# Chunk 3 of both second feed-forward nets by seven block products, with its sums of weights made in DRAM

## The chip, the cores and the metric

The kernel runs on one core of a Trainium2 chip. The metric is the device time of one execution in microseconds; lower is better. [...] In this kernel SP issues most transfers and POOL the accumulating ones, which add what they read to what lies at their destination. Each engine works through its own instructions in the order in which the program put them.

## The reference

Two layers over 256 tokens of width 1024, in 32-bit floats. Each layer runs a feed-forward net, a mixer, a cross attention over 256 memory rows and a second feed-forward net, with a layer norm behind each:

```python
def swiglu(x, w_gate, w_up, w_down):
    return (jax.nn.silu(x @ w_gate) * (x @ w_up)) @ w_down

for l in range(DEPTH):                      # DEPTH = 2, D_FF = 2816
    h = layer_norm(ALPHA * h + 0.5 * swiglu(h, ffn1_gate[l], ffn1_up[l], ffn1_down[l]), ...)
    z = h @ w_in[l]
    ...                                     # gated convolution, linear recurrence, pooling
    h = layer_norm(ALPHA * h + mix, ...)
    h = layer_norm(ALPHA * h + cross_attn(h, mem, ca_q[l], ca_k[l], ca_v[l], ca_o[l]), ...)
    h = layer_norm(ALPHA * h + 0.5 * swiglu(h, ffn2_gate[l], ffn2_up[l], ffn2_down[l]), ...)
```

The change concerns `ffn2`, of both layers: gate and up are 1024 x 2816, down is 2816 x 1024. A part of the mixer's work is issued beside it.

## The kernel before

**Splits.** A product in 32-bit floats is made as three matmuls of a rounded format: each operand is split into a high and a low part, and high x high, high x low and low x high are added up in PSUM. Weights arrive in pieces of 128x1024 (512 KB) in a ring of six buffers `raw`; ScalarE rounds a piece to `whi` (line 75), VectorE subtracts that from it to get `wlo` (line 76). There are eight buffers of each. Activations are split in the same way (`xT`, `kTh`, `ah` and their low parts).

**A feed-forward net** (`ffn`) takes the 2816 columns in six chunks: 0 to 4 are 512 wide, chunk 5 is 256 wide. A chunk makes gate and up for all 256 tokens, the activation and their product, transposes that (`turn`, through a transfer `dealt`), and its rows of `down` follow later in two slabs of 24 matmuls into the accumulators `dn` (`both`). The list `later` says how many slabs stand behind each chunk.

A chunk is made in one of two ways. `hidden` is the plain one: 96 matmuls of 128x512 and eight pieces of weights. `by_seven` cuts tokens and depth into halves, and gate and up into two depth halves each (`w00` = upper half of gate, `w01` = upper half of up, `w10` and `w11` the lower halves), and makes the four results from seven block products of 12 matmuls each instead of eight: X00 by w00, four sums of blocks of x (`bx`, made once for a net) by sums of weight blocks or by a block, X01 by w10 and X11 by a sum of all. It is 84 matmuls, but 14 pieces of weights to split. The sums of weights are made in place, by additions on VectorE (line 702) and by accumulating transfers that POOL issues (`more`, line 738). Where the pieces lie is said by `homes`: two of the blocks use spare buffers, so that they are loaded early, the others the ring `raw`. `put` adds or subtracts a result in PSUM and a tile in SBUF on VectorE, `taken` copies a result by ScalarE, and `between` are slabs of `down` that stand between the products. Which chunks are made so stands in `sevens` (line 821): chunks 2 and 4 in the first net of layer 0, 2, 4 and 5 in the other three.

**The mixer** runs between the first net and the attention. It makes `f`, the keys `k` of the recurrence from it, values, gates, and windows of the pooling (`pw`), whose rims POOL sets to zero (line 1252), and at the end of the recurrence two powers of mean squares `ss` on POOL (line 1219), each followed by a scaled result `yr` (line 1226) that is transposed for the last product of the mixer. In the mixer POOL has nothing else to issue.

What sets the order is the order of the code, apart from `tc.issue_after(x)`, which puts what is written under it behind the instruction x. A transfer waits, on the engine that issues it, for its buffer to be free and for what it reads to be there; what stands behind it in that engine's queue waits with it.

Of the kernel before, what the change touches and what calls it, by code (L numbers as in the profile page):

```python
# [60 lines left out]
def model(ctx: ExitStack, tc: tile.TileContext, t: dict, out: bass.AP):  # L61
# [4 lines left out]
    ps = ctx.enter_context(tc.tile_pool(name="ps", bufs=4, space=PSUM))  # L66

# [257 lines left out]

    squares = kTh[:, 4:8, :].rearrange("p k c -> p (k c)")
# [149 lines left out]
    def ffn(l, name, n, pend=None, last=False, early=None, started=None, following=None):  # L476
        gate, up, down = (t[f"{name}_{x}"][l] for x in ("gate", "up", "down"))
        with tc.tile_pool(name="ffn", bufs=2, reuse_waits="tile") as fp:
# [186 lines left out]
            def by_seven(c0, ncol, bx, between):  # L665
# [22 lines left out]
                if ncol == CHUNK:  # L688
                    homes = [("spare0", "spare1"), ("lng", "lnb"), ("raw", "raw")]
                    n = sevens.index(c0 // CHUNK)  # L690
                    homes = [homes[(n + i) % 3] for i in range(3)] + [("spare2", "raw")]
                else:
                    homes = [("spare2",), ("raw",), ("raw",), ("raw",)]
                w00 = block(gate, 0, pieces(*homes[0]))
                w01 = block(up, 0, pieces(*homes[1]))
                w10 = block(gate, 1, pieces(*homes[3]))
# [23 lines left out]
                def put(o, a, op, b):  # L720
                    nc.vector.tensor_tensor(ordered(o), in_order(a), ordered(b), op=op)
# [18 lines left out]
                o = [bank() for _ in range(3)]  # L740
                run(o[0], part_of_x(0, 0), parts_of(w00))
                taken(s[:, 0, :], o[0])
                run(o[1], bx[0], parts_of(w00, w01))
                more(w01, up, 1)
                run(o[2], part_of_x(0, 1), parts_of(w10))
                between[0]()
                put(s[:, 0, :], o[2], ALU.add, s[:, 0, :])
                w11 = block(up, 1, pieces(*homes[2]))
                run(o[0], bx[1], parts_of(w00, w11), True)
                if ncol == CHUNK:  # L750
                    more(w00, gate, 1)
                copied = taken(e, o[0])
                between[1]()
                nc.scalar.activation(s[:, 0, :], s[:, 0, :], AF.Silu)
                put(e, o[1], ALU.subtract, e)
                if ncol == CHUNK:
                    run(o[0], bx[2], parts_of(w01), True)
                    taken(f, o[0])
                    o.append(bank())
                    run(o[3], bx[3], parts_of(w11))  # L760
                    put(f, o[1], ALU.subtract, f)
                    run(o[0], part_of_x(1, 1), parts_of(w00), True)
                else:
                    o.append(bank())
# [696 lines left out]
```

## Time and profile before

| | |
|---|---|
| median of the runs | 1063.58 us (1063.55 to 1064.38) |
| span of the profiled execution, first to last instruction | 1061.1 us |
| what the median has beyond the span | 2.5 us |
| TensorE busy | 1051.2 us, 99% |
| VectorE busy | 933.2 us, 88% |
| ScalarE busy | 662.0 us, 62% |
| GpSimd busy | 94.7 us, 9% |
| bytes moved by DMA | 251.06 MB, 237 GB/s in the mean |

The second net of layer 0 lies from 372.8 to 539.7 us of the span, that of layer 1 in the last 166 us. In it chunk 2 lies at 406.5 to 435, chunk 3 at 435 to 466, chunk 4 at 466 to 494.5, and chunk 5 with the last slabs at 494.5 to 520.4; these are read from TensorE's matmuls. The mixer of layer 0 lies about 174 to 290 us.

Rows of a timeline read: start, length, engine, line, operation, output<-input with sizes, count, and in brackets the idle time before and what ended it. Rows of a stretch list the busy time of each engine in it, the clock granted to TensorE (1.00 is full speed), the share of time that the DMA engines were busy, and GB/s. Matmuls overlap in the pipeline, so what one costs is the distance between starts, not the listed length.

### The profile page before, as it was taken

The page shows a single profiled execution, that of the slowest core. Times are in us where ns is not written, and L with a number is a line of the kernel's source. Part 1 is how long each engine was busy: PE and PEld are TensorE (multiplying, and loading weights), DVE is VectorE, ACT ScalarE, POOL GpSimd, SP SyncE. Part 2 cuts the span into 40 slices and gives each one's busy share as a digit, 9 for nine tenths or more (in the row PEclk, how much of TensorE's full clock was granted, in tenths as well). Part 3 has the DMA queues.
Part 4 walks back from the last instruction along what each step waited for, and adds up shares of the span by engine and source line. Part 5 has one row for each costly group of instructions (what it writes and reads, how often), then busy time and mean ns, then how long its engine had stood idle before and what let it go on. Part 6 is the DMA issues. An engine that isn't in the chain of part 4 may idle for free.

```text
span 1061.1 us, 16496 instructions
## 1 busy us (share of the span) xinstructions
PE 1051.2 (99%) x6014; PEld 934.8 (88%) x6014; DVE 933.2 (88%) x1246; ACT 662.0 (62%) x909; POOL 94.7 (9%) x128
## 2 busy tenths in 40 slices
PE   9999999999999999999999999999999999999996
PEld 7888888889899888889888888998998998888896
DVE  6998898989988789887898987999899787898787
ACT  6675775676557566655665656666774655675661
POOL 8002001000000001010001001010000000000001
PEclk9999999999999999999999999999999999999999
DMA  9999984854675589988789978866636675799971
GB/s 364 296 320 280 260 272 146 268 166 155 210 271 179 171 281 231 363 192 217 239 305 254 338 224 208 271 233 222 206 122 215 241 243 162 242 303 294 241 194 68
DMA packets 142306, 251.06 MB, mean 237 GB/s; under 512 B 11249, under 2 KB 51985, under 8 KB 142225
## 3 DMA queue, kind: packets, MB, share of 16 engines
q1 hardware_dynamic: 130656, 228.89, 65.0%
q0 software_dynamic: 10992, 19.94, 10.9%
q10 hardware_dynamic: 576, 1.18, 0.3%
q8 instruction: 47, 0.77, 0.3%
q14 instruction: 35, 0.28, 0.1%
HBM read 234.50 MB, written 1.05 MB: 222 GB/s over the span
## 4 chain that ended last, share of the span: by engine, by line
PE 92%; DVE 3%; DMA 2%; issue 2%; ACT 1%; POOL 0%; DVEq 0%; ACTq 0%; POOLq 0%
PE acc L132 61%; PE dn L132 27%; DVE wlo L76 2%; PE acc L199 1%; DMA raw<-in_ffn_gate_dram 1%; DMA raw<-in_ffn_down_dram 1%; ACT whi L75 0%; PE dn L1139 0%; DVE raw L702 0%; PE dn L1213 0%; DMA lng<-in_ln_g_dram 0%; DMA h<-in_x_dram 0%; DVE al L76 0%; PE acc L581 0%; DVE square L531 0%
## 5 line engine op out<-in xcount | busy, mean ns | idle before, releaser
L75 ACT CAST whi<-raw 128x1024 fp32r<-128x1024 f32 (+1 forms) x452 | 456.1, 1042 | 201.2 <-PE dn L132 58.0
L76 DVE TENSOR_TENSOR wlo<-raw,whi 128x1024 fp32r<-128x1024 f32 (+1 forms) x452 | 534.5, 1211 | 53.1 <-ACT whi L75 47.1
L132 PE MATMUL acc<-whi,xT 128*128 128x512 f32 (+1 forms) x1064 | 313.9, 372 | 0.0
L132 PEld LDWEIGHTS acc<-whi,xT 128*128 128x128 f32 x1064 | 199.0, 189 | 26.9 <-DVE xT L76 0.3
L132 PE MATMUL acc<-wlo,xT 128*128 128x512 f32 (+1 forms) x532 | 197.9, 372 | 0.0
L132 PE MATMUL dn<-whi,ah 128*128 128x512 f32 x346 | 131.5, 380 | 0.0
L132 PE MATMUL dn<-wlo,ah 128*128 128x512 f32 x346 | 131.3, 379 | 0.0
L132 PE MATMUL dn<-whi,al 128*128 128x512 f32 x346 | 131.1, 379 | 0.0
L132 PE MATMUL acc<-xT,whi 128*128 128x512 f32 x480 | 117.6, 381 | 0.0
L132 PEld LDWEIGHTS acc<-wlo,xT 128*128 128x128 f32 x532 | 100.6, 189 | 13.4
L132 PEld LDWEIGHTS acc<-xT,whi 128*128 128x128 f32 x480 | 86.8, 190 | 9.8
L132 PE MATMUL dn<-whi,xT 128*128 128x512 f32 x288 | 87.7, 380 | 0.0
L132 PEld LDWEIGHTS dn<-wlo,ah 128*128 128x128 f32 x346 | 65.4, 189 | 9.6 <-DVE wlo L76 0.6
L132 PEld LDWEIGHTS dn<-whi,al 128*128 128x128 f32 x346 | 65.4, 189 | 9.2
L132 PEld LDWEIGHTS dn<-whi,ah 128*128 128x128 f32 x346 | 65.4, 189 | 9.0
L132 PEld LDWEIGHTS acc<-xT,wlo 128*128 128x128 f32 x480 | 62.9, 191 | 3.2
L132 PE MATMUL acc<-xT,wlo 128*128 128x256 f32 x480 | 63.2, 275 | 0.0
L132 PE MATMUL acc<-wlo,kTh 128*128 128x512 f32 (+1 forms) x176 | 61.7, 351 | 0.0
L132 PE MATMUL acc<-whi,kTl 128*128 128x512 f32 (+1 forms) x176 | 61.7, 351 | 0.0
L132 PE MATMUL acc<-whi,kTh 128*128 128x512 f32 (+1 forms) x176 | 61.7, 351 | 0.0
L132 PEld LDWEIGHTS dn<-whi,xT 128*128 128x128 f32 x288 | 54.4, 189 | 7.6
L132 PE MATMUL dn<-wlo,xT 128*128 128x512 f32 x144 | 54.6, 379 | 0.0
(252 smaller groups left out, 1296.8 us busy)
## 6 DMA issues: line engine op xcount, KB each, us to landing
raw<-in_ffn_up_dram SPq DMA_DIRECT2D x88, 512.0 KB, 5.7
raw<-in_ffn_down_dram SPq DMA_DIRECT2D x88, 512.0 KB, 5.6
raw<-in_ffn_gate_dram SPq DMA_DIRECT2D x84, 512.0 KB, 5.6
raw<-in_w_in_dram SPq DMA_DIRECT2D x48, 512.0 KB, 4.8
dealt<-sg SPq DMA_DIRECT2D x80, 128.0 KB, 4.5
raw<-in_ffn_up_dram POOLq DMA_DIRECT2D x19, 512.0 KB, 6.3
raw<-in_ffn_gate_dram POOLq DMA_DIRECT2D x16, 512.0 KB, 9.4
raw<-in_ca_k_dram SPq DMA_DIRECT2D x16, 512.0 KB, 5.2
```

The costliest lines, as they stand in the source:

```text
L75: rounded = nc.scalar.copy(hi, src)
L76: lows.append(nc.vector.tensor_tensor(lo, src, hi.bitcast(F32), op=ALU.subtract))
L132: turns.append(nc.tensor.matmul(o, w, x, start=start, stop=stop, skip_group_check=more))
L199: turns.append(nc.tensor.transpose(pt[:, k, :], src[:, (4 * j + k) * P : (4 * j + k + 1) * P], unit))
```

## The change

Three things are done.

- Chunk 3 of `ffn2` in both layers is made by seven products (`sevens` becomes (2, 3, 4, 5) there). Its four sums of weights (gate0 + up0; up0 + up1; gate0 + up0 + up1; that and gate1) are made in DRAM, in tiles `sum` of 256x512, by transfers that POOL issues: eight copies and four accumulating transfers behind the making of `k` early in the mixer (a small copy `mark` ties them to it), four more behind the memsets of `pw`. In chunk 3 SP then loads 14 pieces, eight of them from `sum`, all by the ring of six. It needs no additions on VectorE and no accumulating transfer of its own.
- In all products by seven X01's product is accumulated by TensorE on top of X00's. ScalarE copies the first product to a second bank, `total`, on which three other products accumulate, and later writes `total` times -1 to a fourth bank, `less`, on which the last sum by w11 accumulates. Two of four additions on VectorE fall away in each; the subtraction f = e - total now reads the bank that TensorE goes on accumulating in.
- In `ffn2` no slab of `down` stands behind a chunk any more (`later` is all 0): the two that stood behind chunk 3 stand inside it. The buffers of chunk 4 in `ffn2` are those that chunk 2 has.

The core of the diff:

```diff
+    def weight_sums(l, name, c):
...
+        def copies():
+            for n, (m, j) in enumerate(((gate, 0), (up, 0), (gate, 0), (gate, 1))):
+                for i in range(2):
+                    nc.gpsimd.dma_start(spread(made[n][i]), part(m, j, i))
+
+        def adds(n):
+            for i in range(2):
+                src = part(up, n, i) if n < 2 else spread(made[n - 1][i])
+                nc.gpsimd.dma_start(spread(made[n][i]), src, accum_op=ALU.add)
+    def after(x, do):
+        mark = sm.tile([P, 8], F32, tag="mark", name="mark", bufs=1)
+        with tc.issue_after(nc.gpsimd.tensor_copy(mark, x).ins):
+            do()
...
+                def summed(n):
+                    to = pieces("raw", "raw")
+                    for x, y in zip(to, stored[n]):
+                        loads.append(nc.sync.dma_start(x, spread(y)))
+                    return to
...
-                    n = sevens.index(c0 // CHUNK)
+                    n = 1 if c0 == 4 * CHUNK and ready is None else 0
...
-                o = [bank() for _ in range(3)]
-                run(o[0], part_of_x(0, 0), parts_of(w00))
-                taken(s[:, 0, :], o[0])
-                run(o[1], bx[0], parts_of(w00, w01))
-                more(w01, up, 1)
-                run(o[2], part_of_x(0, 1), parts_of(w10))
+                o, total, one = (bank() for _ in range(3))
+                run(o, part_of_x(0, 0), parts_of(w00))
+                nc.scalar.copy(total, o)
+                if stored:
+                    run(one, bx[0], parts_of(summed(0)))
+                    w10 = block(gate, 1, pieces(*homes[3]))
+                else:
+                    run(one, bx[0], parts_of(w00, w01))
+                taken(e, one)
+                if not stored:
+                    more(w01, up, 1)
+                run(o, part_of_x(0, 1), parts_of(w10), True)
                 between[0]()
-                put(s[:, 0, :], o[2], ALU.add, s[:, 0, :])
-                w11 = block(up, 1, pieces(*homes[2]))
-                run(o[0], bx[1], parts_of(w00, w11), True)
-                if ncol == CHUNK:
+                activate(s, 0, o)
+                if stored:
+                    run(total, bx[1], parts_of(summed(2)), True)
+                else:
+                    w11 = block(up, 1, pieces(*homes[2]))
+                    run(total, bx[1], parts_of(w00, w11), True)
+                if ncol == CHUNK and not stored:
                     more(w00, gate, 1)
-                copied = taken(e, o[0])
+                less = bank()
+                copied = nc.scalar.mul(less, total, -1.0)
                 between[1]()
...
+                if stored:
+                    run(total, bx[2], parts_of(summed(1)), True)
+                    put(f, e, ALU.subtract, total)
+                    run(less, bx[3], parts_of(block(up, 1, pieces(*homes[2]))), True)
+                    run(total, part_of_x(1, 1), parts_of(summed(3)), True)
+                elif ncol == CHUNK:
+                    run(total, bx[2], parts_of(w01), True)
+                    put(f, e, ALU.subtract, total)
+                    run(less, bx[3], parts_of(w11), True)
+                    run(total, part_of_x(1, 1), parts_of(w00), True)
                 else:
...
+            after(k[:, 0, 0, 0:8], lambda: (ready[1](), ready[2](0), ready[2](1)))
...
+                cleared = nc.gpsimd.memset(x[:, :, 0:PAD], 0.0)
+            with tc.issue_after(cleared.ins):
+                ready[2](2)
+                ready[2](3)
...
+        ready = weight_sums(l, "ffn2", 3)
+        pend = mixer(l, lambda: keys(l, 1), ready)
```

Two places show what moves. The first is GpSimd's queue in the mixer of layer 0; `pw0` and `pw1` are the rims of the pooling windows, `ss` the two powers, `sum` the tiles in DRAM. Before:

```order
L1252 MEMSET pw0_2720 128x2x16
L1219 TENSOR_TENSOR ss_2614<-ss_2614,nhalf_71 128x4
L1252 MEMSET pw1_2721 128x2x16
L1219 TENSOR_TENSOR ss_2660<-ss_2660,nhalf_71 128x4
```

and now, from the last of the accumulating transfers of the first group on (the `mark`, the eight copies and three more of these stand ahead of it):

```order
L351 DMA sum_1811<-in_ffn2_up_dram 128x2x512
L1307 MEMSET pw0_2740 128x2x16
L1274 TENSOR_TENSOR ss_2634<-ss_2634,nhalf_73 128x4
L1307 MEMSET pw1_2741 128x2x16
L351 DMA sum_1812<-sum_1810 128x2x512
L351 DMA sum_1813<-sum_1811 128x2x512
L1274 TENSOR_TENSOR ss_2680<-ss_2680,nhalf_73 128x4
L351 DMA sum_1814<-sum_1812 128x2x512
L351 DMA sum_1815<-sum_1813 128x2x512
```

Two sums of sums now stand between the second memset and the second power; they wait for `sum_1810` and `sum_1811`, which the accumulating transfers of the first group end, and for the copies into their own tiles.

The second is VectorE's queue at the end of chunk 4 of `ffn2` in layer 0, from the splits of the last block on; `halves` holds e and f, the `raw` that is added to is a piece of chunk 5. Before:

```order
L76 TENSOR_TENSOR wlo_4942<-raw_4712,whi_4941 128x1024
L721 TENSOR_TENSOR halves_4725<-acc_4727,halves_4725 128x512
L76 TENSOR_TENSOR wlo_4946<-raw_4713,whi_4945 128x1024
L76 TENSOR_TENSOR wlo_4974<-raw_4963,whi_4973 128x1024
L702 TENSOR_TENSOR raw_4963<-raw_4963,raw_4965 128x1024
L76 TENSOR_TENSOR wlo_4992<-raw_4963,whi_4991 128x1024
L721 TENSOR_TENSOR halves_4725<-acc_4727,halves_4725 128x512
L76 TENSOR_TENSOR wlo_5009<-raw_4967,whi_5008 128x1024
L721 TENSOR_TENSOR halves_4725<-acc_4919,halves_4725 128x512
```

and now:

```order
L77 TENSOR_TENSOR wlo_4991<-raw_4763,whi_4990 128x1024
L77 TENSOR_TENSOR wlo_4995<-raw_4764,whi_4994 128x1024
L77 TENSOR_TENSOR wlo_5023<-raw_5012,whi_5022 128x1024
L747 TENSOR_TENSOR raw_5012<-raw_5012,raw_5014 128x1024
L766 TENSOR_TENSOR halves_4776<-halves_4776,acc_4778 128x512
L77 TENSOR_TENSOR wlo_5041<-raw_5012,whi_5040 128x1024
L766 TENSOR_TENSOR halves_4776<-halves_4776,acc_4911 128x512
```

The first of the three additions to `halves` is gone (ScalarE's copy of e takes its place), and f, the first row of `halves` now, stands behind the two splits of the last block (`raw_4763` and `raw_4764`, to which the accumulating transfers of w00 add), a chunk-5 split and a raw addition, as it did but for one split. It now reads `total`, the bank in which TensorE's last run goes on.

65 lines of the change are left out of this document (34 added, 31 removed).

## The prediction

> **What bounds the kernel now.** I read the page first: the busy times, then the slices, then the chain of work that ended last, then the timelines of single engines in the stage that is changed.
>
> ```profile
> PE 1051.2 (99%) x6014; PEld 934.8 (88%) x6014; DVE 933.2 (88%) x1246; ACT 662.0 (62%) x909; POOL 94.7 (9%) x128
> 372.79 41.44 PE acc L132 x192
> 414.23 5.18 PE dn L132 x24
> 519.21 1.15 DVE wlo L76
> 520.40 7.17 PE dn L132 x32
> ```
>
> The first row says that TensorE is busy for 99% of the span, and VectorE for 88%. The other four are pieces of the chain (start, length, what). In the second feed-forward net of layer 0 the chain runs along TensorE: 192 matmuls in 41.44 us are 0.2158 us each, 24 in 5.18 us are 0.2158 as well. Here a matmul taken out is time taken out, as long as the other engines keep up. The last two rows are the warning: at 519.21 the chain passes to a VectorE subtraction (a `wlo`), and TensorE goes on at 520.40 only when that is done. At the end of this net VectorE delivers just in time.
>
> ```profile
> 406.50:435.00 28.50, 28.50 (x133) 24.95 (x132) 27.31 (x28) 20.23 (x23) 2.38 (x2) 1.00 1.06 317
> 435.00:466.00 31.00, 31.00 (x145) 27.16 (x144) 25.93 (x26) 15.71 (x18) 2.38 (x2) 1.00 0.91 268
> 466.00:494.50 28.50, 28.50 (x135) 24.96 (x134) 22.48 (x22) 18.93 (x21) 3.71 (x3) 1.00 0.81 207
> 494.50:520.40 25.90, 25.85 (x162) 23.33 (x160) 24.88 (x29) 17.39 (x22) 1.45 (x2) 1.00 0.81 245
> ```
>
> These are busy times by stretch: chunks 2, 3, 4 and then chunk 5 with the end (PE, PEld, DVE, ACT, POOL, then the granted clock, the DMA share and GB/s). PE has no idle time in the first three, so nothing but fewer matmuls can shorten them. VectorE is busy for 27.31 + 25.93 + 22.48 + 24.88 = 100.60 of 113.90 us: 13.30 us idle, of which 1.02 in the last stretch.
>
> **The change, part by part.** *Fewer matmuls.* Chunk 3 goes from 96 matmuls of 128x512 to 7 x 12 = 84. 12 x 0.2158 = 2.59 us for a layer, **5.18 us** for two. The other stages have the same matmuls as before.
>
> *VectorE.* It gets six more splits in chunk 3 (14 pieces for 8) and loses two additions of matmul results in each of the existing products by seven.
>
> ```profile
> 468.18 6.89 DVE L76 TENSOR_TENSOR wlo<-raw,whi 128x1024 fp32r<-128x1024 f32 x6
> 474.99 0.68 DVE L721 TENSOR_TENSOR sg<-acc,sg 128x512 f32<-128x512 f32 x1
> 475.59 1.22 DVE L76 TENSOR_TENSOR wlo<-raw,whi 128x1024 fp32r<-128x1024 f32 x1
> 478.85 2.52 DVE L76 TENSOR_TENSOR wlo<-raw,whi 128x1024 fp32r<-128x1024 f32 x2 [2.04 <-ACT whi L75]
> 485.89 2.36 DVE L76 TENSOR_TENSOR wlo<-raw,whi 128x1024 fp32r<-128x1024 f32 x2 [1.83 <-ACT whi L75]
> 497.58 1.22 DVE L779 TENSOR_TENSOR sg<-sg,halves 128x1024 f32<-128x1024 f32 x1
> 499.99 0.42 DVE L721 TENSOR_TENSOR both<-acc,both 128x256 f32<-128x256 f32 x1
> ```
>
> Rows of one engine overlap by 0.08 us (474.99 + 0.68 against 475.59), so six splits from 468.18 to 474.99 are 1.135 us each, a 128x512 addition 0.60, a 128x256 addition 0.34, and the product `sg<-sg,halves` 1.14. In a second net: 6 x 1.135 = 6.81 more for the splits; chunk 3's two gating products (0.60 each) become two additions of the same size and one `sg<-sg,halves`, 1.14 more; chunks 2 and 4 lose two additions each, 2.40, chunk 5 two, 0.68. In sum +4.87 us of work, and 2.59 us less time for it: 105.5 us busy in 111.3, 5.8 idle where 13.3 were. By totals VectorE still keeps up; whether it does at each point is the question. The idle time in the rows above (2.04 and 1.83) was waiting for casts of data that came late, and that remains.
>
> *The tight place: chunk 4.* The subtraction "f = e - total" stands on VectorE behind the two splits of the last block, a chunk-5 split and a raw addition. Much the same stood ahead of it before, but then ScalarE had copied the bank, and no matmul waited for f. Now the last run of twelve matmuls accumulates onto `total` and waits until f has read it, and with it everything behind on TensorE. The other products by seven have the same new wait; in chunk 2 f stands behind three splits of chunk 3 (3.4 us), and two runs of twelve matmuls (5.2 us) cover them if the pieces are there. I leave it at nothing there; if they are not, it costs what they are late. That `o` and `total` are copied by ScalarE before TensorE goes on in them is covered by the twelve matmuls or more between (2.59 us against a copy of 0.6).
>
> ```profile
> 470.84 2.42 POOL L738 DMA_DIRECT2D raw<-in_ffn_gate_dram x2 [14.75 <-DVE wlo L76]
> DMA to landing us min/median/max: 6.0/10.2/12.8
> 478.81 0.38 PE L132 MATMUL acc<-whi,kTh 128*128 128x512 f32 x1
> ```
>
> The two accumulating transfers of w00 are issued from 470.84, the second at 472.05 (half of 2.42 later). From 460 to 500 us such transfers took 6.0 to 12.8 us to land. TensorE starts the second sum's product at 478.81; from there to the last run stand 60 matmuls (12 + 24 + 12 + 12), 12.95 us, so the last run starts at 491.76, or 489.17 after the change. VectorE reaches the issue later than before: chunk 3 costs it 6.81 + 1.14 = 7.95 more and chunk 2 1.20 less, and chunk 3 had 31.00 - 25.93 = 5.07 idle, so up to 1.7 us later, 473.7. That leaves 15.5 us. Needed after the issue are the landing, a cast and two splits (some 3.3), a chunk-5 split, a raw addition and the subtraction (1.14 + 1.14 + 0.60 less overlap): with a landing of 12.8 us 18.2 to 19, with 10.2 some 15.6 to 16, with 6.0 nothing to wait for. So a wait of 0 to 3.5 us for a layer. I take **0.7** for a layer, near the median landing, 1.4 in all. The end of the net, which has no reserve now, is part of this: a VectorE that has caught up in chunk 4 (6.02 idle) enters it as before.
>
> *The bytes of chunk 3.* Six more pieces of 0.52 MB are 3.15 MB; 268 GB/s x 31.0 us = 8.3 MB become 11.5 in 28.4 us, 403 GB/s.
>
> ```profile
> GB/s 364 296 320 280 260 272 146 268 166 155 210 271 179 171 281 231 363 192 217 239 305 254 338 224 208 271 233 222 206 122 215 241 243 162 242 303 294 241 194 68
> raw<-in_ffn_up_dram SPq DMA_DIRECT2D x88, 512.0 KB, 5.7
> ```
>
> No slice of 26.5 us reached that (364 is the highest). Chunk 4 behind it moves only 207 GB/s, so loads fall behind by up to (11.5 - 28.4 x 0.364) / 0.364 = 3 us and catch up there. The cost lies between nothing and those 3 us, as far as pieces are not loaded ahead (ring of six). It falls on the same splits as the wait above, and I count it within the 0.7.
>
> *`less` in chunk 5.* ScalarE now negates `total` between the second sum's product and the last run but two, and only three matmuls (0.65 us) lie between.
>
> ```profile
> 495.89 0.37 ACT L734 COPY both<-acc 128x256 f32<-128x256 f32 x1 [0.74 <-PE acc L132]
> ```
>
> The copy takes 0.37 us, and the matmul before it ends up to 0.16 after the next could start (0.38 against 0.22); with a hand-over at each end that is about 0.65 to 0.9. I take 0.15 for each of three such chunks, **0.45** (0 to 0.8). In the wide chunks 24 matmuls lie there and it costs nothing.
>
> *The sums in DRAM.* In the mixer GpSimd gets a copy, twelve transfers, and later four more.
>
> ```profile
> 196.29 0.41 DVE L993 TENSOR_SCALAR k<-f 128x512 f32<-128x512 f32 x1
> 196.30:251.00 54.70, 54.70 (x594) 49.32 (x593) 48.96 (x94) 37.86 (x68) 1.22 (x3) 1.00 0.66 213
> 239.12 0.13 POOL L1252 MEMSET pw<- 128x32 f32 x1 [60.40 <-ACT half L1019]
> 250.93 0.12 POOL L1252 MEMSET pw<- 128x32 f32 x1 [0.63 <-PE dn L1212]
> 253.52 1.12 POOL L1219 TENSOR_TENSOR ss<-ss,nhalf 128x4 f32<-128x4 f32 x1 [2.47 <-DVE ss L1218]
> 255.78 0.68 DVE L1226 TENSOR_TENSOR yr<-dn,ss 128x512 f32<-128x512 f32 x1
> q1 hardware_dynamic: 130656, 228.89, 65.0%
> q0 software_dynamic: 10992, 19.94, 10.9%
> ```
>
> The twelve begin when `k` is made, 196.7, and at 1.21 us each are issued by 211.2, ahead of the memset at 239.12. The next two, sums of sums, stand between the memset at 250.93 and the second power `ss` at 253.52: their 2.42 us fit into its 2.47 us wait, if the transfers that they wait for have landed by 251. From the last rows a megabyte costs 65.0% x 1061.1 / 228.89 = 3.01 us of all 16 engines by SyncE's queue and 10.9% x 1061.1 / 19.94 = 5.80 by GpSimd's, where mostly accumulations run. Eight copies are 4.19 MB, four additions 2.10. With the copies at 3.01 that is 12.6 + 12.2 = 24.8 us, with all at 5.80 36.5. The loads leave 34% of 54.7 us free, 18.6; where both want the engines I give each half, and then the sums get about 56%, 30.6 us, by 251. So at the lower price they have landed around 240, and at the higher one around 260. The nearest row for a plain copy is q1's, so I take the lower one: nothing for POOL. The loads of the mixer then share with the sums; at 0.66 they have room, and I take **0.4** for both layers (0 to 2). The last sums land long before SyncE loads them at some 435 us, so SyncE waits for nothing new. VectorE's `yr` at 255.78 starts 1.1 us after the power is ready (253.52 + 1.12), the slack before a delay counts.
>
> The Trainium skill speaks against the lower price: "DMA: Bandwidth & Descriptors", in "Latency and other measured facts", gives 207 to 214 GB/s each way for copies from HBM to HBM at full rate. By it the eight copies would take 20 us, an estimate, the sums 32 and not 24.8, and the two layers would lose about 3 us. No row of this case shows a transfer from DRAM to DRAM.
>
> **Sum.** -5.18 + 1.4 + 0.45 + 0.4 = -2.93 us. The profiled span of 1061.1 becomes 1058.2. The median of the runs is 1063.58, 2.5 us more than the span, and I keep that: **1060.7 us**.
>
> **Rivals.** *The saving is eaten in chunks 3 to 5.* VectorE or the loads cannot follow the shorter chunk. For it: the chain at 519.21, the idle time cut to 5.8 us and the 403 GB/s. Against it: 6.02 us of idle time in chunk 4. If the wait is 2.2 us for a layer, about that of a 12-us landing, the time is 1063.58 - 5.18 + 4.4 + 0.85 = 1063.7, no change. *Slower: GpSimd's queue stands still in the mixer.* If the copies cost 5.80 us a megabyte, the first sums land at about 260, the two sums of sums are issued by 262.4, and the second power comes 8.9 us late. Of that 1.1 is slack, 7.8 stands in each layer, since VectorE, which forms `yr`, has no idle time soon after to make it good (8.00 of 8.00 us busy, the row below) and TensorE needs what it makes: 1060.7 + 15.6 = 1076. It decides at 252: a sum that lands earlier costs nothing. In its favour, no row prices a DRAM-to-DRAM transfer, and the window is busy 0.66 already; against it, 55 us are long, and the chain does not pass through GpSimd here.
>
> ```profile
> 262.00:270.00 8.00, 8.00 (x47) 7.25 (x47) 8.00 (x13) 5.15 (x9) 0.00 (x0) 1.00 0.29 81
> 372.80:539.70 166.90, 166.85 (x821) 146.96 (x821) 148.10 (x165) 103.99 (x123) 14.21 (x13) 1.00 0.87 258
> ```
>
> The second row is the whole stage of the second net in layer 0. *Slower in the second nets*: landings of 12.8 us and late loads together, 3.5 to 5 us for a layer, 1065.7 to 1068. *The change does not do what it says*: a hidden load that starves chunk 3 would look like the first rival.
>
> **How the numbers follow.** Forecast 0.46 (1058.8 to 1061.4), saving eaten 0.27 (1061.5 to 1065.6), GpSimd's queue 0.17 (1066 to 1080), slower in the nets 0.10 (1065 to 1069). 0.2%, 2.1 us, is about what a measurement of this kernel can tell from no change. Faster by more: 0.47, within: 0.28, slower: 0.25. The lower end is the whole 5.18 us, 1058.3 (no row shows PE idle time that more could come from). The upper end takes in the nets' rival and the nearer half of the queue's, 1070; beyond lie some 0.12. The forecast's own range is 1058.3 to 1062.
>
> **What would show it.** Right: in the second nets PE's matmuls 12 fewer in chunk 3, the stage 166.9 us long in both layers shorter by 2 us, idle time before PE's last run of chunk 4 under 1 us, and POOL's second `ss` within a microsecond of where it was against its `pw`. Wrong: POOL's DMA issues from sum to sum with a long wait ahead of them and `yr` waiting for `ss`; PE's idle time ahead of chunk 4's last run or at the end above 2 us; loads of `raw<-sum` landing later than ScalarE asks for them; or a mixer that is longer at the same queue position, which would be the shared engines.

## The result and the profile after

| | before | after |
|---|---|---|
| median of the runs | 1063.64 us (1063.55 to 1064.38, four runs) | 1091.4 us (1083.9 to 1093.74, four runs) |
| span of the profiled execution | 1061.1 us | 1089.5 us |

The changed kernel is slower, by a ratio of 1.0247 (95% interval 1.0214 to 1.028). The forecast was 1060.7 us, with a range up to 1070. The runs of after also spread over 10 us, those of before over less than one.

The page of after first, then pieces of its chain of work that ended last (start, length, what). In the rows PE is TensorE (matrix products, with their results in the memory PSUM), PEld the loading of its stationary operand, DVE VectorE, ACT ScalarE, POOL GpSimd and SP SyncE; `raw` and the other loaded tiles lie in the on-chip memory SBUF.

```profile
PE 1059.0 (97%) x5990; PEld 934.4 (86%) x5990; DVE 936.9 (86%) x1238; ACT 673.9 (62%) x927; POOL 127.5 (12%) x162
382.99 36.26 PE acc L133 x168
550.61 36.28 PE acc L133 x168
919.55 36.28 PE acc L133 x168
208.60 19.43 DMA raw<-in_w_in_dram
744.89 21.57 DMA raw<-in_w_in_dram
265.93 6.79 DMA dealt<-yr
799.32 7.04 DMA dealt<-yr
```

TensorE's 24 matmuls fewer are there (5990 for 6014). The chain no longer stays on TensorE: in both mixers it goes through a load of `w_in` that takes some 20 us, and through the transfers of `yr`. The three PE rows mark where the plain chunks of a net start; in the kernel before, the same places are

```profile
539.68 41.44 PE acc L132 x192
895.96 41.44 PE acc L132 x192
```

and 372.79, shown ahead of the result. So the 28.4 us by which the span grew lie as follows:

| stretch | before | after | difference |
|---|---|---|---|
| start to the second net of layer 0 | 372.79 | 382.99 | +10.20 |
| second net of layer 0 | 166.89 | 167.62 | +0.73 |
| first net, mixer and attention of layer 1 | 356.28 | 368.94 | +12.66 |
| second net of layer 1 to the end | 165.14 | 169.95 | +4.81 |

The two nets alone should have come out 2.59 us shorter each, so they lost 3.3 and 7.4 us. Of the other 22.9 us 20.5 are in the two mixers (124.7 and 125.0 us long, where both took 114.6) and some 2.4 in the first net of layer 1. For the mixer of layer 0, the queues (packets, MB, share of the 16 engines) and the issues of transfers (size, median us to landing) from 196.8 to 236 us, before:

```profile
q1 hardware_dynamic: 5226, 8.24, 65.5%
raw<-in_w_in_dram SPq DMA_DIRECT2D x10, 512.0 KB, 4.7
```

and after:

```profile
q0 software_dynamic: 2240, 6.29, 58.4%
q1 hardware_dynamic: 4098, 6.04, 45.3%
raw<-in_w_in_dram SPq DMA_DIRECT2D x10, 512.0 KB, 16.1
sum<-in_ffn_gate_dram POOLq DMA_DIRECT2D x6, 512.0 KB, 13.4
sum<-in_ffn_up_dram POOLq DMA_DIRECT2D x6, 512.0 KB, 18.4
```

Before, the loads took 65.5% of the engines in this stretch; the twelve transfers of the sums take 58.4%, and the two do not fit beside each other. The loads are down to 45.3%, the engines are full, and a load that landed in 4.7 us lands in 16.1. From 250 to 270 us the `dealt<-yr` transfers, 64 KB each, go from 2.2 to 6.1 us beside the last four sums.

How a late load reaches TensorE: ScalarE's casts wait for it (us, times, longest; 196 to 300 us), VectorE has next to nothing to do from 220 to 228 us, and TensorE stops behind them (columns as in the prediction; the clock is third from the end):

```profile
ACT whi L76 <- DMA raw<-in_w_in_dram: 9.8, 3, 5.1
220.00:228.00 8.00, 8.00 (x110) 7.22 (x109) 1.23 (x1) 1.53 (x2) 0.00 (x0) 1.00 1.10 237
228.00:236.00 8.00, 4.68 (x83) 3.81 (x82) 6.24 (x14) 4.64 (x8) 0.00 (x0) 0.92 1.08 305
236.00:244.00 8.00, 8.00 (x64) 7.16 (x66) 5.54 (x15) 5.68 (x13) 0.00 (x0) 0.87 0.75 284
```

Behind the stop the granted clock falls as well: 0.92 and 0.87 over two stretches of 8 us are some 1.7 us of the mixer's 10.1. In layer 1 it fell to 0.82, 0.50 and 0.82 in the three stretches of 4 us from 768 us.

GpSimd's queue in the mixer of layer 0 shows that it isn't where the time goes:

```profile
213.15 1.13 POOL L351 DMA_DIRECT2D sum<-in_ffn_up_dram  x1 [1.43 <-DMA raw<-in_w_in_dram]
257.74 1.04 POOL L1274 TENSOR_TENSOR ss<-ss,nhalf 128x4 f32<-128x4 f32 x1 [13.19 <-DVE ss L1273]
258.75 0.11 POOL L1307 MEMSET pw<- 128x32 f32 x1
258.82 2.33 POOL L351 DMA_DIRECT2D sum<-sum  x2
261.00 1.21 POOL L1274 TENSOR_TENSOR ss<-ss,nhalf 128x4 f32<-128x4 f32 x1
```

The two sums of sums are issued straight after the memset, with no idle time ahead. The first power `ss` is late already, and it waits for VectorE: the loss is made before GpSimd comes to it.

TensorE's waits over the whole span by what ended them (us, times, longest):

```profile
PE dn L1194 <- ACT qc L1143: 6.7, 2, 4.5
PE acc L133 <- DVE halves L766: 6.6, 4, 3.9
PE dn L133 <- DVE wlo L77: 4.3, 9, 0.8
```

The first row is in the two mixers. The waits for f (`halves`) are in the nets: one in the second net of layer 0, one in the first net of layer 1, two in the second net of layer 1. Of the third row 3.6 us lie in the mixers. Now VectorE at the longest wait for f, at the end of chunk 4 in layer 1, with TensorE's clock behind it (busy times by stretch as before, granted clock third from the end):

```profile
1036.58 2.36 DVE L77 TENSOR_TENSOR wlo<-raw,whi 128x1024 fp32r<-128x1024 f32 x2 [3.87 <-ACT whi L76]
1040.12 0.68 DVE L766 TENSOR_TENSOR halves<-halves,acc 128x512 f32<-128x512 f32 x1
1040.00:1044.00 4.00, 3.05 (x7) 2.51 (x8) 3.43 (x5) 3.71 (x4) 1.28 (x1) 0.53 0.35 42
1044.00:1048.00 4.00, 4.00 (x19) 3.48 (x18) 4.00 (x5) 0.78 (x2) 0.00 (x0) 0.62 0.88 176
```

This is the tight place that the prediction named: two splits wait for an accumulating transfer (13.2 us to landing here, 9.8 in layer 0), f stands behind them, and the last run of TensorE behind f. From the issue of the second of these transfers to the time at which the last run was due, 14.0 us passed in layer 0 (486.2 to 500.2) and 14.6 in layer 1 (1022.3 to 1036.9); the prediction had worked out 15.5.

### The profile page after: what moved, and what is told of

Same layout as the page of the kernel before. It is cut to its first block, busy times and chain, and to the rows that moved or that the text cites. A ratio compares the mean times of both kernels' runs of the same rounds, so it can differ in the third digit from the quotient of the medians.

```text
span 1089.5 us, 16527 instructions
## 1 busy us (share of the span) xinstructions
PE 1059.0 (97%) x5990; PEld 934.4 (86%) x5990; DVE 936.9 (86%) x1238; ACT 673.9 (62%) x927; POOL 127.5 (12%) x162
## 4 chain that ended last, share of the span: by engine, by line
PE 74%; DMA 11%; DVE 8%; issue 4%; ACT 2%; POOL 1%; SPq 0%; DVEq 0%; ACTq 0%; POOLq 0%
PE acc L133 49%; PE dn L133 22%; DVE wlo L77 5%; DMA raw<-in_w_in_dram 4%; DMA raw<-in_ffn_gate_dram 3%; DMA raw<-in_ffn_down_dram 2%; DMA dealt<-yr 1%; ACT whi L76 1%; PE acc L200 1%; DMA dealt<-both 1%; DVE raw L747 1%; POOL raw L783 0%; DVE halves L766 0%; DVE yr L1350 0%; DMA h<-in_x_dram 0%
## 5 line engine op out<-in xcount | busy, mean ns | idle before, releaser
L77 DVE TENSOR_TENSOR wlo<-raw,whi 128x1024 fp32r<-128x1024 f32 (+1 forms) x464 | 546.0, 1210 | 66.5 <-ACT whi L76 61.6
L76 ACT CAST whi<-raw 128x1024 fp32r<-128x1024 f32 (+1 forms) x464 | 466.4, 1041 | 206.8 <-DVE raw L747 49.3
L133 PE MATMUL acc<-whi,xT 128*128 128x512 f32 (+1 forms) x984 | 293.0, 375 | 6.6 <-DVE halves L766 6.6
L133 PEld LDWEIGHTS acc<-whi,xT 128*128 128x128 f32 x984 | 185.5, 191 | 33.0 <-issue 5.8
L133 PE MATMUL acc<-wlo,xT 128*128 128x512 f32 (+1 forms) x492 | 183.9, 374 | 0.0
L133 PEld LDWEIGHTS acc<-wlo,xT 128*128 128x128 f32 x492 | 93.9, 191 | 12.4
L133 PEld LDWEIGHTS dn<-wlo,ah 128*128 128x128 f32 x346 | 65.4, 189 | 11.3 <-DVE wlo L77 2.6
L133 PE MATMUL acc<-whi,kTh 128*128 128x512 f32 (+1 forms) x208 | 74.1, 356 | 0.0
L133 PEld LDWEIGHTS dn<-whi,ah 128*128 128x128 f32 x346 | 65.3, 189 | 10.1 <-ACT whi L76 1.4
L133 PE MATMUL acc<-wlo,kTh 128*128 128x512 f32 (+1 forms) x208 | 73.8, 355 | 0.0
L133 PE MATMUL acc<-whi,kTl 128*128 128x512 f32 (+1 forms) x208 | 73.8, 355 | 0.0
L783 POOL DMA_DIRECT2D raw<-in_ffn_up_dram x19 | 23.2, 1228 | 324.2 <-DVE raw L747 188.3
```

The costliest lines, as they stand in the source:

```text
L76: rounded = nc.scalar.copy(hi, src)
L77: lows.append(nc.vector.tensor_tensor(lo, src, hi.bitcast(F32), op=ALU.subtract))
L133: turns.append(nc.tensor.matmul(o, w, x, start=start, stop=stop, skip_group_check=more))
L783: nc.gpsimd.dma_start(x, part_of(m, j, i), accum_op=ALU.add)
```

## The experiments

In five groups; the median of each stands beside that of the kernel before in the same group. Ratios are to the kernel before, with 95% intervals.

### What the sums' transfers cost, and what the wait for f costs

Without the transfers:

```diff
-            [dp.tile([2 * P, CHUNK], F32, ...) for i in range(2)]
-            for n in range(4)
+            [part(m, j, i) for i in range(2)]
+            for m, j in ((gate, 0), (up, 0), (gate, 0), (gate, 1))
...
-                    nc.gpsimd.dma_start(spread(made[n][i]), part(m, j, i))
+            pass
```

> The changed kernel without the sixteen transfers a layer that make the sums in DRAM: chunk 3 loads plain blocks of gate and up in their places, so the sums are left out of its result. Theory A (the sums' transfers crowd the mixer's loads and the dealt transfers): the trace puts 10.1 us in layer 0's mixer and 10.4 in layer 1's on that, so both mixers are back at about 114.6 us and the time is 1091.4 - 20.5 = 1071. Rival B (DRAM to DRAM transfers are harmless, and the mixers are slow from the order of POOL's queue alone): the same, since the queue is back too, so the next group of runs has to part A from B. Rival C (most of the loss comes from the feed-forward nets and varies from run to run): over 1080.

Measured: 1068.15 against 1063.49 us, ratio 1.0057 (1.0028 to 1.0087). 23.2 us of the loss go in the medians (the runs lie between 1065.3 and 1074.8). Layer 0's mixer runs without a gap on TensorE for the 115 us from its start, as before:

```profile
184.30:299.30 115.00, 115.00 (x925) 103.52 (x924) 105.74 (x182) 75.64 (x128) 6.51 (x7) 1.00 0.62 200
```

The second part of the change alone:

```diff
-                stored = ready if c0 == 3 * CHUNK else None
+                stored = None
...
-            sevens = (2, 4) if early is not None else (2, 4, 5) if ready is None else (2, 3, 4, 5)
+            sevens = (2, 4) if early is not None else (2, 4, 5)
```

with `later` and `homes` as before:

> The kernel before with the second part of the change alone: products by seven with X01 accumulated on X00, total and less, two additions on VectorE fewer, f read from the bank that TensorE goes on in; chunk 3 of the second nets as before, no sums. Theory A (this form makes TensorE's last run wait for f, which waits for late accumulating transfers): each wide chunk may lose 0.6 to 4 us when a transfer lands late, 1065 to 1070. Rival D (the waits come from the extra splits in chunk 3 only, the form itself costs at most the 0.45 us of less): 1062 to 1064.5.

Measured: 1063.68 against 1063.49, ratio 1.0002 (0.9992 to 1.0011). No change, Rival D. TensorE's loading waits for `less` in the three products 256 wide are there, and small:

```profile
PEld acc L133 <- ACT acc L807: 0.8, 3, 0.3
```

The changed kernel with f as before:

```diff
-                    put(f, e, ALU.subtract, total)
+                    taken(f, total)
+                    nc.vector.tensor_tensor(ordered(f), ordered(e), ordered(f), op=ALU.subtract)
```

> The changed kernel with total copied by ScalarE for f, as before the change, so that no matmul waits for VectorE's subtraction. Theory A: the four waits for halves (6.6 us in the trace, and some 1.9 us of half clock behind the longest) go but for about 1 us where the split of the late piece itself is waited for: 1091.4 - 7.5 = 1084. Rival E (whatever lands late is waited for anyway, at the splits): within 2 us of 1091.4.

Measured: 1086.14, ratio 1.0209 (1.0188 to 1.023). In the medians 5.3 us go, of the 7.5 expected. But the four runs, 1083.0 to 1087.7, overlap those of the changed kernel, 1083.9 to 1093.7, so a gain from the copy is not shown.

Both edits:

> Both edits together, sums left out of the result as in the first. Theory A: 1091.4 - 20.5 - 7.5 = 1063.4, what is left over the predicted sum being late loads at the ends of the nets (3 to 4 us). If C holds: over 1072. If the prediction's sum for the nets had been right, it would be 1058.4 to 1060.

Measured: 1067.42, ratio 1.0037 (1.0021 to 1.0053). Once the sums are gone the copy is worth 0.7 us, less than these runs spread. In the medians the two edits do not add up (24.0 us together, 23.2 + 5.3 apart); with the changed kernel's spread of 10 us that is not shown. What is clear is that 4 us more than expected stay: with everything taken away that the trace had blamed by name, the kernel is still 4 us slower than with the plain chunk, and 9 us above what 24 matmuls fewer would give (1063.58 - 5.18 = 1058.4).

### Bytes or queue in the mixer; transfers or VectorE in the nets

The mixer first. Only the first twelve transfers:

```diff
-            with tc.issue_after(cleared.ins):
-                ready[2](2)
-                ready[2](3)
```

> The changed kernel without the last four transfers a layer (the sums of sums behind the memsets of pw are left out; chunk 3 takes what the first twelve made). Theory A (each group of transfers crowds what SyncE moves at that time: the first twelve the loads of w_in, the last four the dealt transfers of yr): by the trace the second power is 7.5 us late in layer 0 and the mixer 10.1, so the first group costs some 7.5 and the second 2.6 a layer: 1091.4 - 5.2 = 1086. Rival B (the two sums of sums ahead of the second power hold GpSimd's queue and that makes the loss): the loss goes, about 1070.

Measured: 1086.09 against 1063.38, ratio 1.0207 (1.018 to 1.0234), 5.3 us less in the medians, as theory A had it, though within the spread of the changed kernel; rival B's 1070 is ruled out. Its trace agrees with A: the mixers take 121.0 and 121.6 us, between the 114.6 of before and the 125 of after, and the `dealt<-yr` transfers take 2.2 us again. All sixteen in their places with a sixteenth of the bytes:

```diff
-            [dp.tile([2 * P, CHUNK], F32, ...) for i in range(2)]
+            [dp.tile([16, CHUNK], F32, ...) for i in range(2)]
```

> The changed kernel with all sixteen transfers a layer in their places, with their waits, each of 32 KB and not 512 (chunk 3 loads plain blocks, its result lacks the sums). Theory A (bytes crowd the engines): like the first run, 1068, at most 2 us more. Rival B (the queue, its order and its waits): like the changed kernel, 1085 to 1091.

Measured: 1069.77, ratio 1.0052 (1.0035 to 1.0069). From 190 to 280 us its transfers read

```profile
raw<-in_w_in_dram SPq DMA_DIRECT2D x15, 512.0 KB, 4.9
dealt<-yr SPq DMA_DIRECT2D x8, 64.0 KB, 2.2
```

Both mixers take 114.6 us again, as before the change. So the queue, its order and its waits cost the mixers nothing that the trace shows (the medians of this run and of the one without any sums differ by 1.6 us, within their spread). What costs is the size of the transfers.

Then the nets, both edits on the fourth run of the first group. Six of the fourteen pieces not loaded:

```diff
+                        if n:
+                            nc.gpsimd.memset(x, 0.01)
+                        else:
-                        loads.append(nc.sync.dma_start(x, y))
+                            loads.append(nc.sync.dma_start(x, y))
```

> As the fourth run (no sums made, total copied for f; its result lacks the sums), and six of chunk 3's fourteen pieces are set to a constant by GpSimd, not loaded: the bytes of chunk 3 are those before the change, the fourteen splits stay. Theory A (the nets lose to the transfers: the stretch from chunk 2 to the end kept the 16 engines busy for 0.90 of 113.9 us, 102 us, and six more pieces at 3.0 us a megabyte are 9.4 more, in 111.3): the 8.6 us that the fourth run lies above 1058.8 go almost wholly, 1059 to 1061. Rival D (VectorE's extra splits are what the nets lose to): no change, 1066 to 1067.5.

Measured: 1064.88, ratio 1.0017 (1.0007 to 1.0028): in the medians 2.5 us of 8.6, neither theory (the runs lie between 1063.5 and 1067.8).

Six pieces without a subtraction:

```diff
+                        if rounded:
+                            nc.scalar.copy(h, r[i])
+                            hi.append(h)
+                            lo.append(h)
+                            continue
```

> As the fourth run, with all fourteen pieces loaded, but six of them get no subtraction on VectorE (the rounded part stands in for the low one too, so the result lacks the low parts of three blocks): 6.8 us of VectorE less a net, the transfers as in the fourth run. Theory A (transfers): a part at most, since what comes late still comes late, 1063 to 1067. Rival D (VectorE): 1059 to 1061.

Measured: 1071.03, ratio 1.0063 (1.0043 to 1.0084): 3.6 us slower in the medians, with less to do. Its runs, 1065.7 to 1073.4, overlap those of the fourth run, 1063.6 to 1073.4, so that it is slower is not shown; that it gains nothing like the 6 to 8 us of rival D is. VectorE, ScalarE and the transfers in chunk 3 of layer 0:

```profile
425.00:453.50 28.50, 28.06 (x129) 24.05 (x129) 18.63 (x18) 18.74 (x22) 0.00 (x0) 1.00 1.01 346
```

VectorE is busy for 18.63 of 28.5 us and TensorE loses 0.4 us there all the same. That VectorE has too much work in chunk 3 was my second theory for the nets; it fell here. In the chunk behind it VectorE does run out of idle time. Chunk 4 of the fourth run, VectorE third of the busy times:

```profile
453.50:482.00 28.50, 27.39 (x128) 23.66 (x127) 28.32 (x28) 21.08 (x25) 4.83 (x4) 1.00 1.00 262
```

It is busy for 28.32 of 28.50 us, where chunk 4 had 22.48 before. The 6.02 idle microseconds in which the prediction let it catch up are used up.

### Both reliefs, all pieces, and another place for the sums

Both edits of the last two runs together:

> The fourth run with both reliefs together: six pieces of chunk 3 are set by GpSimd, not loaded, and get no subtraction on VectorE (the result lacks the sums and the low parts of three blocks). Alone the first gave 2.5 of 8.6 us and the second none. Theory F (two limits of like size in chunk 3: pieces that come by a ring of six buffers at 6 to 8 us a landing, and VectorE; taking one away leaves the other): 1059 to 1061. Rival G (neither; the order of waits within a product by seven, or the slabs of down that no longer stand between chunks 3 and 4, is what the nets lose to): 1063 or more.

Measured: 1063.61 against 1063.14, ratio 1.0004 (0.9995 to 1.0014). Two limits that stand in for each other (theory F) would have gone with both; 5 us stay. F fell.

Every piece of chunk 3 set, those of `block` too:

```diff
-                        if n:
+                        if True:
                             nc.gpsimd.memset(x, 0.01)
...
+                        if ready is not None and c0 == 3 * CHUNK:
+                            nc.gpsimd.memset(x, 0.01)
+                            continue
```

> The fourth run with all fourteen pieces of chunk 3 set by GpSimd and none loaded, all fourteen split as usual (the result lacks chunk 3's weights). Theory F: VectorE is the one limit left, and it is not worse than with six set, 1062 to 1065. Rival A (transfers alone, of which six set pieces took too little): 1059 to 1060.5.

Measured: 1063.53, ratio 1.0004 (0.9995 to 1.0014). With no load for chunk 3 at all, 3.9 us of 9 go and no more.

The sums in the attention:

```diff
-            after(k[:, 0, 0, 0:8], lambda: (ready[1](), ready[2](0), ready[2](1)))
...
             query(1, lambda: (weights(0), deal(0), weights(1), deal(1)))
+            after(es[0][:, 0:8], lambda: (ready[1](), ready[2](0), ready[2](1), ready[2](2), ready[2](3)))
```

> The whole computation: the changed kernel with total copied by ScalarE for f, and all sixteen transfers of the sums behind the first softmax numerator of the attention, not in the mixer. Theory A (bytes crowd what SyncE loads at that time): the attention has more idle transfer time from there on (27.7 of 60 us, by the traces of before, against 18.6 of 54.7) but needs 35, so it loses less than the mixer did, 3 to 5 us a layer: 1067.4 + 6 to 10 = 1073 to 1078. Rival H (the place is all that is wrong with the sums): 1067 to 1069. Neither expects it to be faster than before the change.

Measured: 1103.48, ratio 1.0389 (1.0368 to 1.041). Both theories missed it, on the side that says more of crowding: from 322 to 372 us

```profile
dealt<-e SPq DMA_DIRECT2D x16, 64.0 KB, 10.6
sum<-in_ffn_up_dram POOLq DMA_DIRECT2D x6, 512.0 KB, 18.9
```

where the `dealt<-e` transfers took 2.1 us before. These carry the softmax from one product to the next: VectorE waits 17.8 us for them in this layer, 10.6 at the longest, and TensorE stands for 3.7 and 9.0 us behind that. I had worked it out from idle time of the engines in the window; what counted was the time to landing of small transfers that something waits for.

### The form or the arrangement; the reserve

The new form (with the copy for f) under the old arrangement, by the edits of the second and third runs together:

> The kernel before with the new form of the products by seven and total copied by ScalarE for f; chunk 3 plain, no sums. Theory J (the new form makes TensorE wait, through total, less and the copy, once pieces come late): 1064 to 1066, above the 1063.7 of the new form alone. Rival K (the form is harmless; chunk 3's arrangement is what the nets lose to): 1062.5 to 1064.

Measured: 1062.91 against 1063.73, ratio 0.9994 (0.9984 to 1.0003). Of the kernels that compute the whole this is the fastest, but it can't be told from the kernel before.

The old form under the new arrangement, with chunk 3's pieces loaded and then set:

```diff
-                run(o, part_of_x(0, 1), parts_of(w10), True)
+                run(o[2], part_of_x(0, 1), parts_of(w10))
                 between[0]()
-                activate(s, 0, o)
+                put(s[:, 0, :], o[2], ALU.add, s[:, 0, :])
...
+                put(e, o[1], ALU.subtract, e)
```

> Chunk 3 of the second nets by seven as in the changed kernel, with plain blocks for the sums (left out of the result), but all products by seven in the form before the change: four additions on VectorE, total and f copied by ScalarE. Theory J: less than the 1067.4 of the fourth run, 1064 to 1066, though VectorE has 2.4 us more to do in each net's wide chunks. Rival K: 1067 to 1070, the additions on top.

Measured: 1067.01, ratio 1.0029 (1.0016 to 1.0041).

> The same with all fourteen pieces of chunk 3 set by GpSimd and none loaded (chunk 3's weights are left out of the result). Theory J: 1058.5 to 1060.5, the whole saving of 5.2 us. Rival K: 1063 to 1066, as with the new form and all pieces set (1063.5).

Measured: 1064.97, ratio 1.001 (1.0001 to 1.002). Rival K three times: the form is harmless, the arrangement of chunk 3 loses the time, in either form.

The arrangement is three things at once: fourteen pieces of which each serves half as many matmuls, the slabs of `down` inside chunk 3 and not behind it, and other buffers for chunk 4. They were not varied apart. What the traces show is the first, as a reserve. ScalarE's casts of `raw` in chunk 3 say how full the eight buffers of split pieces are: a full ring shows as casts that wait for TensorE to free a buffer. What ended the idle time ahead of the casts (us, times), before:

```profile
  PE acc L132: 7.8, 6
  PE dn L132: 5.9, 3
```

in the fourth run of the first group:

```profile
  DMA raw<-in_ffn_down_dram: 4.4, 4
  DMA raw<-in_ffn_gate_dram: 1.6, 1
  PE acc L133: 0.2, 1
```

and with all pieces set:

```profile
  PE dn L133: 1.5, 2
  PE acc L133: 1.4, 6
```

Before, the ring is full, and a full ring of plain pieces is 8 x 12 matmuls, 20.7 us of work. With all set it is full again, but a piece by seven serves six matmuls, 10.4 us. With all loaded it hardly fills (one wait of 0.2 us). Pairing each subtraction with the first matmul that reads it, split pieces were ready 13.5 to 15.8 us ahead at the end of chunk 3 before (448 to 464 us), 5.0 to 7.4 in after, and 7.9 to 11.3 with all pieces set. What that means for chunk 4 shows in its second accumulating transfer for the last run: before, it was issued 19.7 us ahead of that run (472.05 to 491.76), in the changed kernel 14.0. Taking the accumulating transfers of chunks 4 and 5 away, in three kernels:

```diff
                 def more(to, m, j):
+                    if name == "ffn2" and c0 >= 4 * CHUNK:
+                        return
```

> The run with all fourteen pieces of chunk 3 set, and without the accumulating transfers of chunks 4 and 5 of the second nets (their sums are left out of the result as well). Theory R (the reserve: eight buffers of split pieces hold 20.7 us of TensorE's work in a plain chunk, where a piece serves twelve matmuls, and 10.4 us in a product by seven, where it serves six; so chunk 4, whose accumulating transfers take 6 to 13 us to land, now starts with 8 us of reserve and not 15): with nothing to land the reserve is enough, 1058.5 to 1060.5. Rival K (VectorE's amount of work or something else in chunk 3): 1062.5 to 1064.

Measured: 1061.13 against 1063.25, ratio 0.9983 (0.9974 to 0.9993), 2.4 us less than with them.

> The fourth run (all fourteen pieces loaded) without the accumulating transfers of chunks 4 and 5. Theory R with the loads of chunk 3 as a second loss: 1061 to 1064, 4 to 5 us under the 1067.4 of the fourth run. Rival A (the loads of chunk 3 are all): 1066 to 1067.5.

Measured: 1060.83, ratio 0.9982 (0.9969 to 0.9995), 6.6 us less than with them; the fastest of ten runs was 1058.56.

> The kernel before without the accumulating transfers of chunks 4 and 5 of the second nets. Theory R: its reserve of 15 us covered them, so no change, 1063.4 to 1064. If it gets faster by over 1 us, the first two runs of this group prove less than they seem to.

Measured: 1062.91, ratio 0.9997 (0.9987 to 1.0006). In the kernel before they cost 0.3 us, within its noise; under chunk 3 by seven they cost 6.6. That it isn't their share of the engines is likely, not shown: they are five pieces a net, 2.6 MB, some 15 us of the engines at the prediction's 5.80 us a megabyte, and leaving out 7.3 MB of loads, some 22 us at its 3.01, had given 3.9. That the reserve is what covered them is argued from the casts' waits, the times of issue and these three runs; the reserve itself was not varied. Open stay 2 to 3 us against 1058.4. The traces put part of them into the first net of layer 1. Its code was the same in all variants with the copy; behind a chunk 3 by seven it lost between 0.8 and 3.8 us, in single executions, and behind a plain one, in the first run of this section, only 0.1. Why is open.

## Why the prediction was wrong, point by point

- **Fewer matmuls: right in number and pace, not seen whole in the time.** 24 are gone, and the rest still take 0.216 us each where nothing stops them (168 in 36.28). Without the accumulating transfers of chunks 4 and 5 the median came 2.4 us under the kernel before, and the fastest run 4.0 under its fastest (1058.6 against 1062.6); no run showed the whole 5.18.
- **The sums in DRAM: the step that failed.** The prediction wrote "The loads of the mixer then share with the sums; at 0.66 they have room, and I take 0.4 for both layers (0 to 2)". The other numbers of this step held: 24.8 us of all engines were worked out for the twelve, and 58.4% of 39.2 us, 22.9, were measured; the last of them landed at 235.7 us where 240 had been forecast, and GpSimd issued the next two, at 258.8, without a wait. But that price was only asked whether the sums would be in time. The step had its own warning: the sums need 24.8 us of the engines, and the loads leave 18.6 free. The share that let the sums land by 240 was not charged to the loads. (That share does not come out of "half" either: the free 18.6 us and half of the loads' 36.1 make 36.6 us, 67%, and not 30.6 and 56%. That 58.4% were measured, near the 56, is luck.) The loads paid for it: they land in 16 us and not in 4.7, and ScalarE, VectorE and TensorE wait for them. The two mixers lost 20.5 us by that in the trace, and 23.2 us went with the transfers, not 0.4. The Trainium skill has the rule in "DMA: Bandwidth & Descriptors", "Queues, rings and completion order": each engine takes turns between its queues, packet by packet. The trace fits it, in that both queues moved data side by side (58.4 and 45.3%); it does not show the single turns. The Trainium skill's figure for copies from HBM to HBM in "Latency and other measured facts" of the same page, from which the prediction had estimated 32 us for the twelve, was too dear here: 22.9.
- **GpSimd's queue (the second rival): right that the mixer could be slower, wrong in the mechanism.** It had put a loss behind sums that land after 252. They landed before, and small transfers in the same queue cost nearly nothing. No rival reached 1091, the dearest went to 1080. The last of the prediction's signs of being wrong, "a mixer that is longer at the same queue position, which would be the shared engines", is what came; it had been given no price beyond the 0.4.
- **The tight place in chunk 4: right in mechanism, mis-sized.** "I take 0.7 for a layer, near the median landing" stood against 1.3 us in layer 0 (landing 9.8) and 4.1 in layer 1 (landing 13.2), where half clock behind it took some 3 more (4 us at 0.53, 4 at 0.62). The range for a layer went to 3.5, and half clock was not in it. The term was sized at a landing of 10.2 us; the issue came 14.0 and 14.6 us ahead of the run and not 15.5. How much f itself is worth stays open: 5.3 us in the medians with the sums, 0.7 without, both within the spread of the runs.
- **VectorE's totals: of no use.** They said that VectorE keeps up. It had 10 us idle in chunk 3 when six subtractions were left out, and nothing was gained; and in chunk 4, where 6.02 us of idle time were to make good what came late, it was full. What the change took away was not in a total: a piece by seven is half as much work for TensorE per buffer, so the same eight buffers cover half the time. The prediction counted splits and not how long a full ring lasts. That this is what the nets lost is argued, as said above.
- **The bytes of chunk 3: a real loss, but not alone.** No load at all brings 3.9 us; with chunk 4's accumulating transfers gone, loading them all costs nothing that can be seen (1060.83 against 1061.13).
- **`less` in chunk 5: about as forecast,** 0.45 expected, 0.8 us of waits in the three chunks, and no change in the time of the form alone.

## What to carry to other kernels

A transfer that is hidden behind a busy engine was not free here: it took engine time from transfers that something waited for. So price it by how much later those land, small ones above all, and not by the idle share of the window. When a cheaper product uses each buffer for less work, the same number of buffers covers less time; ask what had lived on that cover. And a saving on the engine that sets the time is only had where the wait that comes next is shorter than the reserve in front of it.

## What the runs showed of the hardware

- A load of 512 KB beside twelve transfers from DRAM to DRAM and accumulations there: 4.7 us in the median without them, 16.1 beside them, 23.2 at most. A 64 KB transfer: 2.1 to 2.2 us without them, 6.1 and 10.6 beside them.
- Copies and accumulations in DRAM, 6.29 MB, kept the 16 engines busy for 22.9 us: 3.6 us a megabyte, less than the 5.8 of the accumulations into SBUF in the kernel before.
- TensorE's granted clock fell behind three waits. After 4.06 us (1036.89 to 1040.95) it was 0.53 and 0.62 in the next two stretches of 4 us, together some 6.8 us at half speed, of which TensorE worked for about 6. After 4.45 us in the mixer of layer 1 it was 0.82, 0.50 and 0.82. In the mixer of layer 0 two waits of 2.30 and 1.02 us, with 32 small matmuls between, were enough for 0.92 and 0.87 in two stretches of 8 us. After single waits of 1.3 us and less in the nets it stayed at 1.00. The Trainium skill, "TensorE: Matmul & The Clock Gate", in "Part 1: The HAM clock gate", puts the fall to half speed behind an idle window of about 3.4 us and the return behind about 3.4 us of sustained work. The waits of 4.06 and 4.45 us agree with the first; behind the two shorter waits the clock fell without a single idle stretch of 3.4 us, and the return took some 6 us of work here.
